# One TensorE queue in source order, reset visit delays, fixed PSUM banks, and both heads of a product in one visit

## The chip, the cores and the metric

One core of one Trainium2 chip runs the whole program. The metric is device time in microseconds (us): the median of several executions. TensorE (PE in the rows) has two records for each product, the weight load (PEld) and the matmul; the other engines are VectorE (DVE), ScalarE (ACT), GpSimd (POOL) and SyncE (SP), which issues most of the DMAs.

## The reference, cut to what matters

One layer of a streaming encoder: two groups of heads on one combined projection, and an output projection.

```python
xn = rms_norm(x, norm_g)
proj = xn @ w_in                       # 2048 x 8320: q, k, v, gates, RWKV rows
q, k = rope(rms_norm(q)), rope(rms_norm(k))
o = softmax(mask(q1 k1)) v - lam * softmax(mask(q2 k2)) v   # two maps a head, 8 heads
for t in tokens:                       # RWKV-7 recurrence, 16 heads of 64
    S = S * w_t + (S a_t) b_t + v_t k_t
    y_t = S r_t
out = concat(att_out, rw_out) @ w_out  # 2048 x 2048
return x + out, k, v, S, last row
```

It is computed for 1024 new frames (64 frames to a chunk) and for 32 frames of a running stream with 256 frames of past.

## The kernel before, in words

The tokens are worked in two halves: A has 544 columns (512 new frames and the 32 of the running stream, projected as 288 + 256 columns), B has 512. For each half there are eight units; unit u is one attention head and one pair of recurrence heads. A unit has eight projections (`proj`, lines 354 to 381): q, k, v, attention gate, three recurrence rows, recurrence gate. Each is 16 blocks of the contraction by three products (`wh xh`, `wh xl`, `wl xh`, which together stand for fp32), so 96 matmuls in A and 48 in B. Ahead of each half stand one norm (`rb_a`, `rb_b`) and one small projection (`lora`). Behind the 16 units come the 16 output projections of A and the 16 of B. All of this is written into the PSUM tag `pj` with three banks.

Everything else runs as *visits* to TensorE between these matmuls. Six streams (lines 167 to 168) are Python generators: `chs` (the recurrence chunk by chunk, `rw_chain`), `dns` (what it needs, `rw_down`), `qks` (norms of q and k, transposes of v), `pos` (`rw_post`), `ats` (`att_task`) and `los` (`rw_decay`). While it writes the program, the planner keeps a clock (`clk`) of the TensorE time it has issued; a stream yields a delay, looked up in the table `LAT` (line 39), and its next visit is written as soon as the clock has passed that delay and one of the stops is reached: `pump()` after every twelve matmuls of a projection in A and six in B, `chs.run()` after every three. `ready` holds a second due time for the shared banks `am` and `Y`. `drain(stream, name)` writes nothing but visits until the named task is through; where none is due it moves its clock on. After the first projection of a unit stands `drain(ats, ("att", u - 1))`: the attention of the unit before must be through. The same is done for the q, k and v tasks one projection after each was added, for `down` and `vread` in the recurrence rows and for the last tasks ahead of the sixteenth output projection.

In the program thus written every engine's order is still open: the Tile scheduler sorts each engine's instructions by the order of the source and by when they are ready in its own timing, TensorE's among them. A delay that is too short in the source therefore costs little: other matmuls are put in front. Each visit allocates its PSUM tile anew from the tags `am`, `Y`, `sc` and `ch`.

The places that the steps below touch: the product BK*AR (lines 753 to 768), for each chunk and head a fp32 matmul of 64 rows by 128 columns of weights and 128 columns of data, two passes each; four chunks of one head make a visit into the bank `Y`. The chunk step (lines 886 to 908): visit c1 `ch<-Sw,AR`, then `RS` (ACT) and `xs` (DVE) from its bank, visit c2 `ch<-xs,TT`, then two copies to `UV`, visit c3 `ch<-UV,MM`, then the new state. Attention in A (`att_task`, `att_finish`): for each of four blocks of queries scores, transposes (`sc<-cst,E`), the product with v (`am<-Vt,E`), and the closing transpose (`am<-cst,os`); then for the running stream `smp0` (`am<-E,qb`), `smp1` (`am<-cmb,E`), `smp2` (`am<-E`) and a last closing transpose.

Of the kernel before, what the change touches and what calls it, by code (L numbers as in the profile page):

```python
# [12 lines left out]
F32R = mybir.dt.float32r  # L13
# [24 lines left out]

LAT = dict(qkA=6246, qkB=2980, vA=9930, vB=9930, finA=1949, finB=3111, sc1A=1400, sc1B=1260, scAA=3566, scAB=3056, sc2A=3181, sc2B=3736, aTA=640, aTB=873, smp0A=2190, smp0B=3000, smp1A=4433, smp1B=7243, smp2A=1452, smp2B=1100, decA=3192, decB=6684, rnA=2646, rnB=1890, msA=8290, msB=8364, ms2A=2463, ms2B=1016, bk0A=1758, bk0B=1724, att0A=4044, att0B=1900, am2A=304, am2B=265, Y2A=1822, Y2B=1994, boA=1350, boB=3075, bktA=2250, bktB=2000, ttA=13941, ttB=14740, t10A=2258, t10B=1343, c0A=1052, c0B=2447, c1A=2162, c1B=1936, c2A=1122, c2B=978, c3A=1014, c3B=1276, postA=6000, postB=4636, dmA=5550, dmB=4110, solveA=31509, solveB=33325, am=900, Y=2208, scA=5863, sc1=2240, sc2=2872)
P3B = 3  # L40
# [6 lines left out]
def build(tc, I, O):  # L47
# [16 lines left out]
    clk = [0.0]  # L64
    ready = {"am": 0.0, "Y": 0.0}

    def am():
        ready["am"] = None
        return PT("am", 1)

    def ym():
        ready["Y"] = None
        return PT("Y", 1)

# [7 lines left out]

    def mm(out, lhsT, rhs, start=True, stop=True):
        n, m = 1, 1
        for d in rhs.shape[1:]:
            n *= d
        for d in lhsT.shape[1:]:
            m *= d
        shaped(lhsT.shape[0], m)
        load = 0.83 * m + 5.0  # L90
        clk[0] += max(0.4375 * n + 6.0, load) if rhs.dtype == F32R else 2 * max(0.84 * n, load)
        PE.matmul(out, lhsT, rhs, start=start, stop=stop)  # L92
# [11 lines left out]
    class Stream:  # L104
# [11 lines left out]
        def due(self):  # L116
            if self.cur is None and not self.q or self.cond is not None and not self.cond():
                return None
            return max(self.at, ready[self.am]) if self.am else self.at

# [5 lines left out]
        def step(self):  # L126
            if self.cur is None:
                if not self.q:
                    return False
                self.cur = self.q.pop(0)  # L130
            if self.cond is not None and not self.cond():
                return False
            if self.due() > clk[0]:
                return False
            self.cond, self.am = None, None
            try:
                y = next(self.cur[1])
            except StopIteration:
                self.done.add(self.cur[0])
                self.cur = None  # L140
                y = 0
            for r in ready:
                if ready[r] is None:
                    ready[r] = clk[0] + LAT[r]
            if callable(y):
                self.cond = y
            elif isinstance(y, tuple):
                self.at, self.am = clk[0] + y[0], y[1]
            else:
                self.at = clk[0] + y  # L150
            return True
# [256 lines left out]
    def lat(key, half):  # L408
        return LAT[key + "AB"[half]]
# [107 lines left out]
    def att_task(half, h, st):  # L517
# [9 lines left out]
        for j in range(4):  # L527
# [10 lines left out]
            if half == 0:  # L538
                sc = PT("sc", 1, (128, 2, 512))
                for c in range(2):  # L540
# [8 lines left out]
            else:  # L549
                for c in range(2):  # L550
                    if c:
                        yield lat("sc1", half) + 2 * nk
                    sc = PT("sc", 1, (128, 2, 512)).rearrange("p a b -> p (a b)")
                    scores(sc, c, qc, segs)
                    V.memset(sc[0:64, nk - 64:nk], NEG)
                    V.tensor_reduce(mx[:, c:c + 1], sc[:, :nk], AX.X, ALU.max)
                    V.tensor_scalar(mx[:, c:c + 1], mx[:, c:c + 1], -SCALE, None, ALU.mult)
                    S.activation(E[c][:, :nk], sc[:, :nk], AF.Exp, bias=mx[:, c:c + 1],
                                 scale=SCALE, accum_out=l[:, c:c + 1])
# [7 lines left out]
            aT = T([128, 8, 128], "E1")  # L567
            pt = PT("sc", 1, (128, 8, 128))
            for kb in range(nb):
# [148 lines left out]
    def rw_down(half, i, sub, st):  # L718
# [35 lines left out]
        for c0 in range(0, cn, 4):  # L754
            m = min(4, cn - c0)
            for h in range(2):
                yield lat(key, half), "Y"
                key = "ms2"
                hr = (low, high)[h]
                p = ym()  # L760
                for j in range(m):
                    mm(p[:, 128 * j:128 * j + 128],
                       BK[hr, c0 + j].rearrange("p a t -> p (a t)"),
                       AR[hr, c0 + j].rearrange("p a t -> p (a t)"))
                V.tensor_tensor(MM[:, c0:c0 + m, h, :].rearrange("p c (x t) -> p c x t", t=64)[:, :, 0:3:2, :],  # L765
                                p[:, :128 * m].rearrange("p (a x t) -> p a x t", x=2, t=64),
                                mask.rearrange("p (x t) -> p x t", x=2).unsqueeze(1).to_broadcast([128, m, 2, 64]),
                                op=ALU.mult)
# [24 lines left out]
        for c0 in range(0, cn, 4):  # L793
            m = min(4, cn - c0)
            yield lat("ms2", half), "Y"
            p = ym()
            for j in range(m):
                tr(p[:, 128 * j:128 * j + 128], BK[:, c0 + j].rearrange("p a t -> p (a t)"), ident)
            for h in range(2):
                S.copy(MM[:, c0:c0 + m, h, 64:128],  # L800
                       p[:, :128 * m].rearrange("p (a b) -> p a b", b=128)[:, :, 64 * h:64 * h + 64])
# [11 lines left out]
    def rw_chain(half, i, sub, st):  # L813
# [8 lines left out]
        yield lat("bk0", half)  # L822
        p = PT("ch", 1)
        for j in range(2):
# [22 lines left out]
        yield max(1500, t_m + lat("tt", half) - clk[0])  # L847
        p = PT("ch", 1)
        for g in range(ng):
            mm(p[32:64, 32 * g:32 * g + 32], MMg[0:32, g, 32:64], u0[:, g, :])  # L850
        S.copy(wt, p[32:64, :32 * ng].rearrange("p (a b) -> p a b", b=32))
        yield lat("t10", half)
        p = PT("ch", 1)
        for g in range(ng):
            mm(p[0:32, 32 * g:32 * g + 32], wt[:, g, :], t01[32:64, g, :])
        pg = p[0:32, :32 * ng].rearrange("p (c h b) -> p c h b", h=2, b=32)
        for h in range(2):
            S.copy(TT[64 * h:64 * h + 32, :, 64 * h + 32:64 * h + 64], pg[:, :, h, :])
        yield lat("t10", half)
        p = PT("ch", 1)  # L860
        for c in range(cn):
# [16 lines left out]
        for c in order:  # L878
# [10 lines left out]
            key = "c1"  # L889
            ch = PT("ch", 1)  # L890
            mm(ch[:, 0:128], AR[:, c].rearrange("p a t -> p (a t)"), Sf)
            RS = T([128, 128], "RS")
            S.copy(RS[high], ch[high, 0:128])  # L893
            xs = T([128, 64], "xs")
            for h in range(2):
                V.tensor_tensor(xs[64 * h:64 * h + 64], ch[low, 64 * h:64 * h + 64], MM[low, c, h, 0:64], op=ALU.add)  # L896
            SP = T([64, 2, 64], "SP")
            for h, hr in enumerate((low, high)):
# [261 lines left out]
```

## Time and profile before

| | us |
|---|---|
| median of 3 runs | 2612.56 (2609.12 to 2618.03) |
| profiled execution | 2613.46 |
| span of its profile | 2611.7 |
| PE busy in it | 2549.7 |
| DVE busy | 1892.0 |
| ACT busy | 1349.6 |

The page gives busy time by engine; a record of a matmul reaches about 0.2 us past the point where the next one begins, so that the distance of two starts is what a matmul costs in a stream. "Idle before" counts only what lies between the end of one record and the start of the next, so a delay shorter than that overhang doesn't show.

### The profile page before, as it was taken

The numbers are of one execution on the slowest core, as the hardware profiler recorded it, in microseconds if no ns is written. First come the engines' busy times: TensorE is split into PE (matmuls) and PEld (weight loads), VectorE is DVE, ScalarE is ACT, GpSimd is POOL, SyncE is SP. The second block draws the span as 40 slices with busy tenths as digits, with TensorE's granted clock in tenths as the row PEclk, the third lists the DMA queues.
The fourth block names the chain that finished last, engine by engine and source line by source line (L and its number), as shares of the span: only waits on it lengthen the run. The fifth ranks groups of instructions, "written<-read, shape, count | busy, mean of one in ns | idle before, by whom it ended". The sixth has DMA issues, their size and how long they took to land. (4 is left out here: it accounts for less than half of the span.)

```text
span 2611.7 us, 49090 instructions
## 1 busy us (share of the span) xinstructions
PE 2549.7 (98%) x17128; PEld 2220.1 (85%) x17128; DVE 1892.0 (72%) x5768; ACT 1349.6 (52%) x3138; POOL 415.1 (16%) x949
## 2 busy tenths in 40 slices
PE   7999999999999999999999999999999999999999
PEld 7999999999898999877777777777777778999887
DVE  7576877777777787788787887788878888753432
ACT  6455555555555655565555555555555556332321
POOL 3211111111111111111111111111111111111000
PEclk9999999999999999999999999999999999999999
DMA  4433332324242524353332323232324244544443
GB/s 156 119 102 94 93 103 84 110 82 115 75 122 80 170 72 122 98 153 100 98 98 87 103 83 106 85 111 81 114 81 115 77 132 118 176 148 140 137 142 108
DMA packets 198665, 286.74 MB, mean 110 GB/s; under 512 B 102097, under 2 KB 115921, under 8 KB 198417
## 3 DMA queue, kind: packets, MB, share of 16 engines
q0 software_dynamic: 51088, 169.12, 21.8%
q1 hardware_dynamic: 147328, 114.47, 15.5%
q8 instruction: 136, 2.23, 0.4%
q14 instruction: 113, 0.92, 0.1%
HBM read 228.11 MB, written 37.51 MB: 102 GB/s over the span
## 5 line engine op out<-in xcount | busy, mean ns | idle before, releaser
L92 PE MATMUL pj<-xh,wh 128*128 128x256 f32 (+2 forms) x3888 | 1294.2, 333 | 7.7 <-ACT xh L248 6.7
L92 PE MATMUL pj<-xl,wh 128*128 128x256 f32 (+2 forms) x3888 | 1274.7, 328 | 5.0 <-DVE xl L249 5.0
L92 PE MATMUL pj<-xh,wl 128*128 128x256 f32 (+2 forms) x3888 | 1272.5, 327 | 1.1 <-DVE wl L225 1.1
L92 PEld LDWEIGHTS pj<-xh,wh 128*128 128x128 f32 x3888 | 735.7, 189 | 61.2 <-ACT xh L248 7.0
L92 PEld LDWEIGHTS pj<-xl,wh 128*128 128x128 f32 x3888 | 736.2, 189 | 52.5 <-DVE xl L249 8.8
L92 PEld LDWEIGHTS pj<-xh,wl 128*128 128x128 f32 x3888 | 735.4, 189 | 52.4 <-DVE wl L225 2.1
L224 ACT CAST wh<-wr 128x512 fp32r<-128x512 f32 x584 | 360.6, 618 | 471.8 <-PE pj L92 420.1
L225 DVE TENSOR_TENSOR wl<-wr,wh 128x512 fp32r<-128x512 f32 x584 | 401.2, 688 | 193.5 <-ACT wh L224 162.9
L231 POOL DMA_DIRECT2D wr<-w_in x517 | 278.3, 538 | 1639.8 <-DVE wl L225 492.2
L786 DVE TENSOR_TENSOR ts<-tm,ts 64x54 f32<-64x54 f32 (+35 forms) x992 | 198.2, 200 | 15.1
L784 DVE TENSOR_TENSOR tm<-ts,ms 64x54 f32<-64x54 f32 (+35 forms) x992 | 197.7, 199 | 14.5 <-DMA ts<-tinit 0.2
L92 PEld LDWEIGHTS ch<-UV,MM 64*64 64x64 f32 (+2 forms) x1632 | 111.5, 145 | 38.1 <-DVE UV L903 9.2
L92 PE MATMUL ch<-UV,MM 64*64 64x64 f32 (+2 forms) x1632 | 128.9, 231 | 8.0 <-DVE UV L846 5.1
L899 ACT ACTIVATE SP<-Sw,PL 64x64 f32<-64x64 f32 x256 | 88.3, 345 | 91.2 <-DVE Sw L908 78.1
L225 DVE TENSOR_TENSOR wl<-MM,wh 128x512 fp32r<-128x512 f32 x64 | 44.0, 689 | 89.1 <-ACT wh L224 89.1
L224 ACT CAST wh<-MM 128x512 fp32r<-128x512 f32 x64 | 39.6, 620 | 128.9 <-PE pj L92 123.3
L896 DVE TENSOR_TENSOR xs<-ch,MM 64x64 f32<-64x64 f32 x272 | 58.6, 216 | 50.2 <-ACT RS L893 45.7
L908 DVE SCALAR_TENSOR_TENSOR Sw<-ch,PL,SP 64x64 f32<-64x64 f32 x256 | 70.7, 276 | 23.2 <-PE ch L92 16.7
L92 PE MATMUL am<-Vt,E 128*128 128x128 f32 (+1 forms) x592 | 84.7, 280 | 1.8 <-ACT wh L224 1.1
L92 PE MATMUL Y<-AR,BK 64*128 64x128 f32 x544 | 84.8, 290 | 0.7 <-DVE MM L765 0.6
L92 PEld LDWEIGHTS Y<-AR,BK 64*128 64x128 f32 x544 | 67.5, 188 | 19.8 <-issue 9.1
L92 PEld LDWEIGHTS am<-Vt,E 128*128 128x128 f32 (+1 forms) x592 | 73.5, 189 | 8.7 <-issue 2.6
(303 smaller groups left out, 3127.9 us busy)
## 6 DMA issues: line engine op xcount, KB each, us to landing
wr<-w_in POOLq DMA_DIRECT2D x517, 256.0 KB, 3.2
wr<-w_out POOLq DMA_DIRECT2D x64, 256.0 KB, 3.6
MM<-w_out POOLq DMA_DIRECT2D x32, 512.0 KB, 4.0
t<-xB SPq DMA_DIRECT2D x32, 256.0 KB
ms<-dm SPq DMA_DIRECT2D x96, 64.0 KB
t<-t SPq DMA_DIRECT2D x64, 68.0 KB
t<-mixd SPq DMA_DIRECT2D x16, 272.0 KB
t<-xA SPq DMA_DIRECT2D x16, 272.0 KB
```

The lines of the kernel that those rows point to most:

```text
L92: PE.matmul(out, lhsT, rhs, start=start, stop=stop)
L224: S.copy(wh, raw)
L225: V.tensor_tensor(wl, raw, wh.bitcast(F32), op=ALU.subtract)
L231: q.dma_start(raw, wsrc[:, g * 512:(g + 1) * 512].rearrange("p (k f) -> p k f", k=4))
L784: V.tensor_tensor(tm, ts_[:, 0:qn, s:s + 1].to_broadcast([R * nb, qn, m]), ms[:, s:s + 1, s + 1:32].to_broadcast([R * nb, qn, m]), op=ALU. ...
L786: V.tensor_tensor(ts_[:, 0:qn, s + 1:32], tm, ts_[:, 0:qn, s + 1:32], op=ALU.add)
L896: V.tensor_tensor(xs[64 * h:64 * h + 64], ch[low, 64 * h:64 * h + 64], MM[low, c, h, 0:64], op=ALU.add)
L899: S.activation(SP[:, h, :], S_[hr, h, :], AF.Copy, scale=PL[hr, 0, gc:gc + 1])
L908: V.scalar_tensor_tensor(S_[hr, h, :], ch[low, 192 + 64 * h:256 + 64 * h], PL[low, h, gc:gc + 1], SP[:, h, :], ALU.mult, ALU.add)
```

## The change

TensorE gets its instructions in the order of the source (`tc.manual_schedule` for PE alone); the other engines are sorted as before. The table of delays is reset: most grow, a few shrink, and there are new entries for two steps that had shared one. The banks `am`, `Y`, `sc` and `ch` are allocated once and kept. BK*AR takes both heads in one visit: the matmuls alternate between rows 0 to 63 and rows 64 to 127, head 0 into `Y` and head 1 into `am`; the planner counts them at half the time. In the chunk step `xs` is now written ahead of `RS`.

```diff
-LAT = dict(qkA=6246, qkB=2980, vA=9930, vB=9930, finA=1949, finB=3111, sc1A=1400, sc1B=1260, scAA=3566, scAB=3056, sc2A=3181, sc2B=3736, aTA=640, aTB=873, smp0A=2190, smp0B=3000, smp1A=4433, smp1B=7243, smp2A=1452, smp2B=1100, decA=3192, decB=6684, rnA=2646, rnB=1890, msA=8290, msB=8364, ms2A=2463, ms2B=1016, bk0A=1758, bk0B=1724, att0A=4044, att0B=1900, am2A=304, am2B=265, Y2A=1822, Y2B=1994, boA=1350, boB=3075, bktA=2250, bktB=2000, ttA=13941, ttB=14740, t10A=2258, t10B=1343, c0A=1052, c0B=2447, c1A=2162, c1B=1936, c2A=1122, c2B=978, c3A=1014, c3B=1276, postA=6000, postB=4636, dmA=5550, dmB=4110, solveA=31509, solveB=33325, am=900, Y=2208, scA=5863, sc1=2240, sc2=2872)
+LAT = dict(qkA=6246, qkB=2980, vA=9930, vB=9930, finA=3400, finB=3400, sc1A=1400, sc1B=2600, scAA=6400, scAB=3056, sc2A=3181, sc2B=4100, aTA=1200, aTB=2000, smp0A=3600, smp0B=3000, smp1A=9000, smp1B=7243, smp2A=1452, smp2B=1100, decA=3192, decB=6684, rnA=2646, rnB=6200, msA=8290, msB=8364, ms2A=2600, ms2B=3000, bk0A=7300, bk0B=6000, att0A=4044, att0B=1900, am2A=2100, am2B=265, Y2A=1950, Y2B=1950, boA=1350, boB=3075, ttA=27000, ttB=25500, t10A=1000, t10B=1000, c0A=1300, c0B=1700, c1A=2500, c1B=2300, c2A=2500, c2B=2500, c3A=1700, c3B=1800, postA=6000, postB=4636, dmA=5550, dmB=4110, solveA=31509, solveB=33325, am=1500, Y=2208, scA=5863, sc1=2240, sc2=2872, x0A=1000, x0B=1000, bkA=2600, bkB=3000)
...
+    held = {}
+
+    def bank(tag, shape=(128, 512)):
+        if tag not in held:
+            held[tag] = PT(tag, 1, shape)
+        return held[tag]
+
     def am():
         ready["am"] = None
-        return PT("am", 1)
+        return bank("am")
...
-        clk[0] += max(0.4375 * n + 6.0, load) if rhs.dtype == F32R else 2 * max(0.84 * n, load)
+        clk[0] += (max(0.4375 * n + 6.0, load) if rhs.dtype == F32R else 2 * max(0.84 * n, load)) / ways
...
         for c0 in range(0, cn, 4):
             m = min(4, cn - c0)
+            yield lat(key, half), "Y", "am"
+            key = "ms2"
+            ps2 = (ym(), am())
+            for j in range(m):
+                for h, hr in enumerate((low, high)):
+                    mm(ps2[h][:, 128 * j:128 * j + 128],
+                       BK[hr, c0 + j].rearrange("p a t -> p (a t)"),
+                       AR[hr, c0 + j].rearrange("p a t -> p (a t)"), ways=2)
             for h in range(2):
-                yield lat(key, half), "Y"
-                key = "ms2"
-                hr = (low, high)[h]
-                p = ym()
-                for j in range(m):
-                    mm(p[:, 128 * j:128 * j + 128],
-                       BK[hr, c0 + j].rearrange("p a t -> p (a t)"),
-                       AR[hr, c0 + j].rearrange("p a t -> p (a t)"))
                 V.tensor_tensor(MM[:, c0:c0 + m, h, :].rearrange("p c (x t) -> p c x t", t=64)[:, :, 0:3:2, :],
...
-            ch = PT("ch", 1)
+            ch = bank("ch")
             mm(ch[:, 0:128], AR[:, c].rearrange("p a t -> p (a t)"), Sf)
-            RS = T([128, 128], "RS")
-            S.copy(RS[high], ch[high, 0:128])
             xs = T([128, 64], "xs")
             for h in range(2):
                 V.tensor_tensor(xs[64 * h:64 * h + 64], ch[low, 64 * h:64 * h + 64], MM[low, c, h, 0:64], op=ALU.add)
+            RS = T([128, 128], "RS")
+            S.copy(RS[high], ch[high, 0:128])
...
     with tile.TileContext(nc) as tc:
-        build(tc, I, O)
+        with tc.manual_schedule(engines={mybir.EngineType.PE}):
+            build(tc, I, O)
```

## Rows read from the trace of the kernel before

**Rows 1.** The page: the span, and busy time by engine.
```profile
span 2611.7 us, 49090 instructions
PE 2549.7 (98%) x17128; PEld 2220.1 (85%) x17128; DVE 1892.0 (72%) x5768; ACT 1349.6 (52%) x3138; POOL 415.1 (16%) x949
```
**Rows 2.** Busy time by stretch: length, PE, PEld, DVE, ACT, POOL, granted clock, DMA share, GB/s.
```profile
0.00:37.20 37.20, 24.54 (x121) 21.30 (x122) 29.95 (x47) 22.84 (x37) 16.66 (x27) 0.86 0.61 205
22.00:31.00 9.00, 7.90 (x32) 7.24 (x32) 8.68 (x9) 2.61 (x5) 4.55 (x4) 0.50 0.16 50
40.00:60.00 20.00, 18.92 (x143) 17.81 (x141) 10.39 (x19) 14.85 (x23) 3.60 (x9) 1.00 0.37 107
```
**Rows 3.** Timeline of PE around one visit: start us, length us.
```profile
2236.06 0.29 PE L92 MATMUL pj<-xh,wl 128*128 128x288 f32 x1
2236.28 1.16 PE L92 MATMUL Y<-AR,BK 64*128 64x128 f32 x8
...
2237.61 0.30 PE L92 MATMUL pj<-xl,wh 128*128 128x288 f32 x1
2237.75 0.29 PE L92 MATMUL pj<-xh,wl 128*128 128x288 f32 x1
```
**Rows 4.** Groups by line and form: busy us, mean ns | idle before, by releaser.
```profile
L92 PE MATMUL Y<-AR,BK 64*128 64x128 f32 x544 | 84.8, 290 | 0.7 <-DVE MM L765 0.6
L92 PE MATMUL ch<-xs,TT 128*128 128x64 f32 x272 | 54.3, 281 | 12.2 <-DVE xs L896 7.0 <-issue 2.1 <-ACT E L571 1.1
```
**Rows 5.** Timeline of PE, a visit whose products use two column halves.
```profile
631.00 0.68 PE L92 MATMUL ch<-UV,MM 64*64 64x64 f32 x16
```
**Rows 6.** Timeline of PE around a chunk visit that waits.
```profile
700.27 0.28 PE L92 MATMUL pj<-xh,wl 128*128 128x256 f32 x1
700.62 0.46 PE L92 MATMUL ch<-Sw,AR 128*128 128x128 f32 x2
```
**Rows 7.** What VectorE waited for ahead of `xs`: us, times.
```profile
  ACT RS L893: 47.8, 42
```
**Rows 8.** Timeline of PE at the start.
```profile
21.66 0.61 PE L92 MATMUL pj<-xl,wh 128*128 128x288 f32 x1 [2.29 <-DVE xl L249]
...
37.23 0.62 PE L92 MATMUL am<-asg,p 128*128 128x272 f32 x2
```
**Rows 9.** Timeline of DVE at the start.
```profile
32.17 0.69 DVE L225 TENSOR_TENSOR wl<-wr,wh 128x512 fp32r<-128x512 f32 x1 [1.49 <-ACT wh L224]
35.51 0.72 DVE L273 TENSOR_TENSOR asg<-asg,p 128x544 f32<-128x544 f32 x1
```
**Rows 10.** Timeline of PE, end of attention in a unit of A, and the projection behind.
```profile
563.81 0.25 PE L92 MATMUL am<-kb,qb 128*64 128x32 f32 x2
573.12 0.81 PE L92 MATMUL am<-cmb,E 64*128 64x32 f32 x6
581.90 0.24 PE L97 MATMUL am<-cst,os 32*128 32x32 f32 x1
583.59 0.29 PE L92 MATMUL pj<-xh,wh 128*128 128x288 f32 x1
```
**Rows 11.** Timeline of DVE, what `smp1` there needs.
```profile
565.63 0.45 DVE L595 TENSOR_REDUCE sx<-am 64x1 f32<-64x288 f32 x1
568.24 0.29 DVE L602 TENSOR_SCALAR cmb<-cst,sx,cvec 64x32 f32<-64x32 f32 x1
```
**Rows 12.** Timeline of ACT, what the last closing transpose there needs.
```profile
576.70 0.27 ACT L504 ACTIVATE os<-am 32x128 f32<-32x128 f32 x1 [0.62 <-PE am L92]
577.65 0.36 ACT L509 ACTIVATE os<-am,sm 32x128 f32<-32x128 f32 x1
```
**Rows 13.** Timeline of PE, end of attention in a unit of B.
```profile
1558.48 1.95 PE L92 MATMUL am<-Vt,E 128*128 128x128 f32 x16
1563.26 0.27 PE L97 MATMUL am<-cst,os 128*128 128x128 f32 x1
```
**Rows 14.** Instructions of the norm ahead of half B: ns min/median/max, first and last start.
```profile
L92 PE MATMUL am<-p,p x8: 270/274/377, 1144.3 to 1147.6; 128*128 128x128 f32 x8
```

More of the change, by code (lines that the diff above doesn't have):

```diff
@@ L65, in build, with scores2 @@
     ready = {"am": 0.0, "Y": 0.0}
+    held = {}
[3 more added lines that the diff above has]
+        return held[tag]
     def am():
         ready["am"] = None
-        return PT("am", 1)
+        return bank("am")
     def ym():
         ready["Y"] = None
-        return PT("Y", 1)
+        return bank("Y")
+    def scores2():
+        return bank("sc", (128, 2, 512))
     mode = [(128, 128)]
@@ L81, in shaped, with mm @@
             mode[0] = now
-    def mm(out, lhsT, rhs, start=True, stop=True):
+    def mm(out, lhsT, rhs, start=True, stop=True, ways=1):
         n, m = 1, 1
@@ L118, in due @@
                 return None
-            return max(self.at, ready[self.am]) if self.am else self.at
+            return max(self.at, *(ready[a] for a in self.am)) if self.am else self.at
         def run(self):
@@ L147, in step @@
             elif isinstance(y, tuple):
-                self.at, self.am = clk[0] + y[0], y[1]
+                self.at, self.am = clk[0] + y[0], y[1:]
             else:
@@ L538, in att_task @@
             if half == 0:
-                sc = PT("sc", 1, (128, 2, 512))
+                sc = scores2()
                 for c in range(2):
@@ L552, in att_task @@
                         yield lat("sc1", half) + 2 * nk
-                    sc = PT("sc", 1, (128, 2, 512)).rearrange("p a b -> p (a b)")
+                    sc = scores2().rearrange("p a b -> p (a b)")
                     scores(sc, c, qc, segs)
@@ L567, in att_task @@
             aT = T([128, 8, 128], "E1")
-            pt = PT("sc", 1, (128, 8, 128))
+            pt = scores2().rearrange("p a (b t) -> p (a b) t", t=128)
             for kb in range(nb):
@@ L755, in rw_down @@
             m = min(4, cn - c0)
-            for h in range(2):
-                yield lat(key, half), "Y"
-                key = "ms2"
-                hr = (low, high)[h]
-                p = ym()
-                for j in range(m):
-                    mm(p[:, 128 * j:128 * j + 128],
-                       BK[hr, c0 + j].rearrange("p a t -> p (a t)"),
-                       AR[hr, c0 + j].rearrange("p a t -> p (a t)"))
+            yield lat(key, half), "Y", "am"
[6 more added lines that the diff above has]
+                       AR[hr, c0 + j].rearrange("p a t -> p (a t)"), ways=2)
+            for h in range(2):
                 V.tensor_tensor(MM[:, c0:c0 + m, h, :].rearrange("p c (x t) -> p c x t", t=64)[:, :, 0:3:2, :],
-                                p[:, :128 * m].rearrange("p (a x t) -> p a x t", x=2, t=64),
+                                ps2[h][:, :128 * m].rearrange("p (a x t) -> p a x t", x=2, t=64),
                                 mask.rearrange("p (x t) -> p x t", x=2).unsqueeze(1).to_broadcast([128, m, 2, 64]),
@@ L794, in rw_down @@
             m = min(4, cn - c0)
-            yield lat("ms2", half), "Y"
+            yield lat("bk", half), "Y"
             p = ym()
@@ L822, in rw_chain @@
         yield lat("bk0", half)
-        p = PT("ch", 1)
+        p = bank("ch")
         for j in range(2):
@@ L847, in rw_chain @@
         yield max(1500, t_m + lat("tt", half) - clk[0])
-        p = PT("ch", 1)
+        p = bank("ch")
         for g in range(ng):
@@ L852, in rw_chain @@
         yield lat("t10", half)
-        p = PT("ch", 1)
+        p = bank("ch")
         for g in range(ng):
@@ L858, in rw_chain @@
             S.copy(TT[64 * h:64 * h + 32, :, 64 * h + 32:64 * h + 64], pg[:, :, h, :])
-        yield lat("t10", half)
-        p = PT("ch", 1)
+        yield lat("x0", half)
+        p = bank("ch")
         for c in range(cn):
```

## The prediction

> **What bounds the kernel now.** I read the page first, then busy time by stretch, then TensorE's groups by form, then the timeline around single visits. The page says that TensorE is busy for 2549.7 of 2611.7 us [rows 1], so the end of the kernel is TensorE's own queue: every matmul taken out of it and every wait in it counts in full, and every wait put into it as well. The other engines (DVE 72%) matter by when they release a visit. TensorE is idle for 62.0 us in all [rows 1]; the first 37.2 us hold 12.7 of that, since it is busy for 24.54 there [rows 2]. The other 49.3 us lie in short waits at visits. That is less than what they cost: at 700.27 a projection matmul starts, the visit behind it at 700.62 [rows 6], where the mean distance in a dense stretch is 18.92 / 143 = 0.132 us [rows 2]; of the 0.22 us lost, the record of the matmul (0.28 us long) leaves only 0.07 visible as idle. So visits come a little too early as a rule, and the sorted queue hides the rest by putting projection matmuls in front.
>
> **BK*AR, both heads in one visit.** From the last projection matmul before a visit to the second behind it, 2236.06 to 2237.61, are 1.55 us; two of these matmuls cost 2 x 0.14, so the visit costs 1.27 us [rows 3]. With eight passes at some 0.115 us (first to last start is 1.16 less a record's 0.29, seven gaps of 0.12 [rows 3, 4]) that leaves 0.35 us for going in and out. The 544 passes [rows 4] are 64 visits of eight and 16 of two (subs of 4 and 5 chunks in A, 4 and 4 in B). After: 32 of sixteen and 8 of four. Whether row halves run side by side no row of before shows, as each visit used one half. The nearest row is a visit that uses two column halves: 16 passes in 0.68 us, less a record's overhang of some 0.2, are 0.03 us each [rows 5], where 64 columns alone would cost half of 0.115, 0.058; there two passes do run at once. I take that for row halves too: a double visit then costs what a single one does and some 0.1 more, so 32 x 1.17 + 8 x 0.5 = **-42 us**. If they don't, only the entries are saved: 40 x 0.35 = -14. The Trainium skill, TensorEngine Tiling (Array Packing), section PSUM Pressure, says that different row tiles must not write one PSUM bank at the same time; the change uses two banks, as that asks. No run here shows that rule, and the sum doesn't use it.
>
> **Source order and later visits.** With TensorE in source order the planner's delays decide. The new ones for the chunk steps (c1 2.5, c2 2.5, c3 1.7 in A) are longer by 0.3 to 1.4 us, and `xs` no longer stands behind `RS`, for which VectorE waited 47.8 us in 42 cases [rows 7]. The recurrence has room for that: it isn't what the projections wait for, as the wait on `xs` in front of TensorE is 12.2 us in 272 passes [rows 4]. So most of the 49.3 us of idle time behind the start goes, and the hidden part (0.15 us in perhaps 170 of the 408 chunk visits, 25 us) pays for the visits that are still late, which now hold the whole queue. I take **-50 us**; bounds -25 (half stays) and -75 (both go). The banks that are kept cost nothing: the same readers must be through before the next write; that holds unless the kept tile brings a second semaphore wait, which is inside these bounds.
>
> **The start.** `rb_a` stands ahead of all projections in the source. In the trace its first matmul runs at 37.23 [rows 8], behind 121 projection matmuls that the sorter put in front [rows 2]. In source order TensorE waits for the last sum of squares, 35.51 + 0.72 = 36.23 [rows 9], and then has those 121 to do: 121 x 0.132 = 16.0 us. It can start 0.8 us earlier than 37.23, or 4.7 if the weight casts, one of which ran ahead of the last sums after a wait of 1.49 us [rows 9], are held back by full buffers. So +11 to +15, and up to 4.5 more (half of the 9.00 us at clock 0.50 [rows 2]) if it starts at the lower of its two levels, 1.2 GHz. I take **+14**. `rb_b` has four rounds of matmul, copy, same bank, spread over 1144.3 to 1147.6 [rows 14] among other matmuls; alone in the queue they cost 3.3 less 8 x 0.11 = **+2.5** (0 to 3).
>
> **The drain of attention.** This is the price of the change. In a unit of A the last closing transpose is at 581.90 and the next projection begins at 583.59 [rows 10]: attention ends 1.7 us ahead of the drain point as it is. The new table adds 4 x 2.83 (scA) + 5 x 1.45 (fin) + 1.41 + 4.57 (smp0, smp1) + 4 x 0.56 (aT) = 26.8 us to its delays. Some 25 us of planned delays then fall behind the drain point, so `smp0`, `smp1`, `smp2` and the last closing transpose stand in the queue with no projection between. TensorE doesn't wait for the planned time there but for the data. For `smp1` that took from 564.06 to 568.53 = 4.5 us with a loaded VectorE [rows 10, 11] (its visit came at 573.12, 9.1 us later, for want of the bank), and for a closing transpose from 576.70 to 578.01 = 1.3 us [rows 12]; `smp0` has its data already; `smp2`, two small copies, I estimate at 0.5. That is 6.3 us; chunk visits that the drain lets through fill some of it. I take 4.5 us of idle time a unit, bounds 2 and 12 (9.1 and a loaded 2.8). Eight units: **+36** (16 to 96). In B the closing transpose is at 1563.26 [rows 13], at the drain point, and the table adds 4 x (1.34 + 0.36 + 1.13 + 0.29) = 12.5 us: the last product and closing transpose fall behind it. Between these lay 1563.26 - 1560.43 = 2.8 us [rows 13], at best 1.3 [rows 12]; with part of the wait ahead of the product I take 2.5 a unit (1.3 to 5), seven units, **+17.5** (9 to 35). What is queued behind is the q evacuation and all projections; no other engine has work that needs TensorE meanwhile.
>
> **The sum**, against the profiled execution's 2613.46 us (0.9 above the median): -42 - 50 + 14 + 2.5 + 36 + 17.5 = -22, so 2591.5; I say **2591**.
>
> **The rivals.**
> The drains cost more, and the kernel is slower: with 12 us a unit in A and 4 in B they take 96 + 28 = 124 in place of 53.5, and the time is 2661. It decides at the point where the drains eat the gain, 92 - 16.5 = 75.5 us over 15 drains, 5.0 us each. For it: closing transposes and `smp1` waited that long in this trace, and chunk visits in between have waits of their own. Against it: the long ones were queues on VectorE and ACT that a standing TensorE doesn't feed. Clock: after an idle 2.29 us at 21.66 [rows 8] the granted clock was 0.50 from 22 to 31 us [rows 2]; a fall like that in each drain of A would add 8 x 4.5 = 36, so 2697. The Trainium skill, TensorE: Matmul & The Clock Gate, section HAM oscillation, warns of just this, of idle time between bursts that throttles the clock again and again; the stretch from 22 to 31 us agrees.
> Row halves don't overlap: -14 in place of -42, 2619.
> The waits all go and the drains are nearly free, because attention, no longer queued behind early work, comes in time: -42 - 75 + 14 + 16 + 9 = -78, 2535.
> The sorted order was near the source's anyway, so that the order itself changes nothing: then only the merged visits count, 2571; it is part of the forecast's range.
>
> **How the numbers follow.** Forecast (2555 to 2604): 0.40. Nearly free drains (below 2555): 0.13. No overlap (near 2619): 0.13. Costly drains (above): 0.34. About 0.3%, 8 us, is what a measurement of this kernel can tell from no change: faster 0.40 + 0.13 = 0.53, same 0.13, slower 0.34. Cases of both signs hold the chance, so the range takes in both: 2530 (all waits gone, drains at their lower bound) to 2685 (costly drains, some lower clock); the forecast's own range is 2555 to 2604.
>
> **What would show it.** BK*AR: visits of sixteen passes, some 1.4 us from first start to the next projection, not 2.1. Source order: idle ahead of `ch` visits down from what it is, `rb_a` as TensorE's first matmuls, at 32 to 37 us. Drains: in each unit a stretch of some 10 us after the first projection in which TensorE runs only visits, with `am<-cmb,E`, `am<-E` and `am<-cst,os` the ones that wait, 4 to 6 us idle in A and 2 to 3 in B; and the granted clock there. Wrong would be: attention through ahead of the drain point; idle time in a drain above 5 us; passes of the two halves starting 0.11 us apart.

## The result, and the profile after

The changed kernel takes 2826.07 us (median of 4 runs, 2821.76 to 2828.24) where the kernel before takes 2612.64 beside it (2609.12 to 2618.03): a ratio of 1.081, interval 1.079 to 1.084. It is slower by 213 us. The forecast was 2591 and the range ended at 2685, so size and sign were both wrong.

The page of the changed kernel: span, busy time by engine, then TensorE's busy share and its granted clock in 40 equal slices, in tenths.

```profile
span 2822.7 us, 48865 instructions
PE 2544.6 (90%) x17128; PEld 2262.1 (80%) x17128; DVE 1915.7 (68%) x5768; ACT 1349.0 (48%) x3138; POOL 422.6 (15%) x949
PE   4989898998989798988989898989898989899999
PEclk9989899998989898989999999999899999999999
```

TensorE does the same 17128 matmuls and is busy as long as before, 2544.6 against 2549.7 us [rows 1]. Its idle time went from 62.0 to 2822.7 - 2544.6 = 278.1 us, which is more than the whole difference. In the busy time two things nearly cancel: the merged visits take time out, and the granted clock, 0.943 on the mean where it was 0.995, puts time in. The same matmuls with the same merged visits are busy for 2519.5 us at clock 0.988 in the run `merged_sorted` below, so some 25 us here may be the clock's (an estimate from these two runs). The dips in the first row come once a unit. One of them, in the busy time by stretch (length, PE, PEld, DVE, ACT, POOL, granted clock, DMA share, GB/s): the start, the 16 us ahead of the second projection of unit 4, that place itself, the 14 us behind it, and the same place in a unit of B.

```profile
0.00:37.20 37.20, 3.52 (x9) 2.70 (x9) 28.48 (x46) 21.81 (x35) 14.53 (x24) 1.00 0.54 184
615.00:631.00 16.00, 15.38 (x126) 15.17 (x126) 12.43 (x40) 9.11 (x23) 1.66 (x4) 1.00 0.35 90
631.00:651.00 20.00, 10.26 (x50) 6.88 (x49) 18.31 (x72) 8.80 (x26) 1.50 (x5) 0.64 0.18 55
651.00:665.00 14.00, 14.00 (x103) 14.00 (x103) 5.10 (x19) 4.04 (x11) 1.08 (x2) 0.91 0.42 108
1999.00:2020.00 21.00, 9.95 (x44) 8.23 (x43) 17.22 (x66) 9.30 (x25) 0.74 (x2) 0.65 0.30 91
```

For 20 us TensorE runs 50 matmuls and is busy half the time, while VectorE is busy 18.31 us. The granted clock is 0.64 there, a mixture of its two levels, 1.2 and 2.4 GHz. The timeline of TensorE in that drain (start, length, and in brackets the idle time ahead and what ended it):

```profile
631.14 0.28 PE L102 MATMUL pj<-xh,wl 128*128 128x256 f32 x1
632.75 0.33 PE L107 MATMUL am<-cst,os 128*128 128x128 f32 x1 [1.33 <-ACT os L519]
634.35 0.64 PE L107 MATMUL am<-cst,Yt 128*128 128x128 f32 x3 [1.27 <-DVE asg L524]
...
636.10 0.25 PE L102 MATMUL am<-kb,qb 128*64 128x32 f32 x2
...
639.05 1.27 PE L102 MATMUL am<-cmb,E 64*128 64x32 f32 x6 [2.06 <-DVE tm L794]
642.72 0.55 PE L102 MATMUL Y<-AR,BK 64*128 64x128 f32 x1 [2.40 <-DVE ts L796]
...
646.28 1.06 PE L102 MATMUL am<-E 128*32 128x128 f32 x4 [1.34 <-DVE MM L775]
...
650.47 0.31 PE L107 MATMUL am<-cst,os 32*128 32x32 f32 x1 [0.38 <-DVE MM L775]
650.71 0.61 PE L102 MATMUL pj<-xh,wh 128*128 128x288 f32 x1
```

From the last matmul of the first projection to the first of the second are 19.6 us. Adding up the idle time between these two matmuls gives 4.7 to 12.0 us in each of the 15 drains, 139 in all, and 7.5 more behind the last projection of A, around the norm `rb_b`; in the kernel before no idle time shows at these places. The start has 33.7. The remaining 98 us lie ahead of visits inside the units. TensorE's waits by releaser (us in total, times, longest), the largest first:

```profile
PE am L107 <- DVE Yt L947: 35.3, 18, 3.9
PE am L102 <- DVE p L317: 33.7, 1, 33.7
PE ch L102 <- ACT RS L906: 30.7, 20, 4.7
PE am L107 <- ACT os L519: 22.3, 15, 3.6
PE ch L102 <- DVE UV L913: 21.4, 11, 3.7
PE sc L107 <- DVE tm L794: 20.0, 6, 3.6
PE Y L102 <- DVE ts L796: 17.0, 6, 3.2
```

And two of TensorE's groups, which answer to [rows 4] (busy, mean ns, idle before by releaser):

```profile
L102 PE MATMUL Y<-AR,BK 64*128 64x128 f32 x272 | 52.9, 340 | 20.5 <-DVE ts L796 17.0 <-DVE MM L775 1.9 <-DVE BK L760 1.5
L102 PE MATMUL ch<-xs,TT 128*128 128x64 f32 x272 | 48.9, 262 | 30.8 <-ACT RS L906 30.7
```

The waits are spread over recurrence, attention and what precedes it, with no single line to blame. Where `xs` waited behind `RS` on VectorE before, it now waits for TensorE (35.3 us in 32 cases), and the product behind it waits for `RS`: 30.8 us of idle time where it was 12.2. (Of the 47.8 us in [rows 7] 45.7 were VectorE's, in 40 cases; the other 2.1 lay ahead of TensorE's weight load.)

### The profile page after: what moved, and what is told of

It reads as the page before. It is cut to its first block, busy times and chain, and to the rows that moved or that the text cites. A ratio compares the mean times of both kernels' runs of the same rounds, so it can differ in the third digit from the quotient of the medians.

```text
span 2822.7 us, 48865 instructions
## 1 busy us (share of the span) xinstructions
PE 2544.6 (90%) x17128; PEld 2262.1 (80%) x17128; DVE 1915.7 (68%) x5768; ACT 1349.0 (48%) x3138; POOL 422.6 (15%) x949
## 4 chain that ended last, share of the span: by engine, by line
PE 69%; DVE 18%; ACT 6%; issue 4%; DMA 2%; POOL 0%; SPq 0%; DVEq 0%; ACTq 0%; POOLq 0%
PE pj L102 54%; PE ch L102 5%; PE am L102 4%; DVE wl L235 3%; DVE ts L796 2%; DVE tm L794 2%; PE Y L102 2%; PE sc L102 1%; PE sc L107 1%; PE am L107 1%; ACT wh L234 1%; DVE E L573 1%; DVE t L472 1%; DVE Sw L918 1%; PE Y L107 1%
## 5 line engine op out<-in xcount | busy, mean ns | idle before, releaser
L102 PE MATMUL pj<-xh,wh 128*128 128x256 f32 (+2 forms) x3888 | 1332.1, 343 | 3.4 <-DVE t L361 3.4
L102 PEld LDWEIGHTS pj<-xh,wl 128*128 128x128 f32 x3888 | 744.4, 191 | 58.0 <-DVE wl L235 0.4
L102 PEld LDWEIGHTS pj<-xh,wh 128*128 128x128 f32 x3888 | 746.1, 192 | 51.9 <-DVE t L361 4.3
L102 PEld LDWEIGHTS pj<-xl,wh 128*128 128x128 f32 x3888 | 746.7, 192 | 40.7
L794 DVE TENSOR_TENSOR tm<-ts,ms 64x54 f32<-64x54 f32 (+35 forms) x992 | 198.5, 200 | 18.6 <-DMA Qd<-Qd 1.0
L796 DVE TENSOR_TENSOR ts<-tm,ts 64x54 f32<-64x54 f32 (+35 forms) x992 | 198.5, 200 | 18.1
L102 PE MATMUL am<-Vt,E 128*128 128x128 f32 (+1 forms) x592 | 94.0, 311 | 5.5 <-DVE ts L796 3.1
L102 PEld LDWEIGHTS am<-Vt,E 128*128 128x128 f32 (+1 forms) x592 | 85.2, 220 | 13.7 <-issue 9.5
L904 DVE TENSOR_TENSOR xs<-ch,MM 64x64 f32<-64x64 f32 x272 | 58.6, 215 | 39.9 <-PE ch L102 35.3
L102 PEld LDWEIGHTS ch<-xs,TT 128*128 128x128 f32 x272 | 46.3, 192 | 42.9 <-ACT RS L906 38.4
L568 ACT ACTIVATE E<-sc,sm 128x640 f32<-128x640 f32 (+3 forms) x64 | 61.1, 954 | 37.9 <-DVE sm L567 37.3
```

The costliest lines, as they stand in the source:

```text
L794: V.tensor_tensor(tm, ts_[:, 0:qn, s:s + 1].to_broadcast([R * nb, qn, m]), ms[:, s:s + 1, s + 1:32].to_broadcast([R * nb, qn, m]), op=ALU. ...
L796: V.tensor_tensor(ts_[:, 0:qn, s + 1:32], tm, ts_[:, 0:qn, s + 1:32], op=ALU.add)
```

## The experiments

Three theories stood against each other. **O**: the fixed order itself costs the time; whatever a visit waits for, TensorE now waits too. **P**: the new, longer delays cost it, by pushing attention past the drain point. **Q**: in the drains TensorE stands behind VectorE's queue, above all the 62 operations of each triangular solve. Times without an interval are those of one execution; the kernel before had 2609.6 to 2619.0 us beside them.

**Order and delays apart.** Four kernels: only the order held; the whole change with the old delays; the whole change with the order left to the scheduler; and the last with the old delays as well.

```diff
     with tile.TileContext(nc) as tc:          # order_alone: this edit in the kernel before
-        build(tc, I, O)
+        with tc.manual_schedule(engines={mybir.EngineType.PE}):
+            build(tc, I, O)
-LAT = dict(... c1A=2500 ...)                  # old_delays: this edit in the changed kernel
+LAT = dict(... c1A=2162 ...)                  # all old values; x0 as t10, bk as ms2
```

> The kernel before with TensorE in source order and nothing else. Theory P: the plan of before has next to no empty time, so 2640 to 2720 us: the start costs 15, early visits cost the rest. Rival O: 2800 or more. Against the run with old delays it shows what kept banks and merged visits give in source order: 30 to 45 us by the prediction's term.

> The whole change but for the table: source order on TensorE, kept banks, both heads in one visit, and the delays of before (the two new entries at the values they shared). Theory P (the lengthened delays plan empty time into the drains, and source order makes TensorE stand there): the fifteen stretches of some 20 us behind each first projection shrink to a few us and most of the loss goes, 2600 to 2690 us, while visits that now come too early wait. Rival O (source order itself costs, whatever the delays, since no other matmul can be put in front of a wait): the time stays near 2800.

> The whole change with the new delays, but TensorE sorted by the scheduler as before. Theory P: the sorter puts projection matmuls into the drains, so the time is near or below before, 2570 to 2630 us. If the long delays cost by themselves (attention late whoever orders it), 2700 or more.

> Kept banks, both heads of BK*AR in one visit and xs ahead of RS, with the sorted order and the delays of before. The prediction's term for the merged visits is -42 us if the row halves overlap and -14 if not: 2570 or 2599 us.

Measured: order alone 2870.9; whole change with old delays 2828.4; whole change without the order 2654.4; that with old delays 2604.8 (median of 10 executions, ratio 0.9975, interval 0.9962 to 0.9988). The order costs 2870.9 - 2612.6 = 258 us on the kernel before, 2828.4 - 2604.8 = 224 on the changed one with old delays and 2826.1 - 2654.4 = 172 with the new ones. The new delays cost 2654.4 - 2604.8 = 50 us where the order is sorted and nothing (-2) where it is held. So O holds and P doesn't. The 50 us of the new delays in sorted order were not followed up. The page of the whole change without the order:

```profile
span 2652.6 us, 48829 instructions
PE 2527.5 (95%) x17128; PEld 2220.1 (84%) x17128; DVE 1894.3 (71%) x5768; ACT 1344.8 (51%) x3138; POOL 419.6 (16%) x949
```

Its idle time is 125.1 us where the changed kernel has 278.1. So of the 170 us between the two spans 153 are idle time and 17 are busy time, at a mean clock of 0.943 in place of 0.974. Where the waits are does depend on the table. With the old delays the drains, the one behind the last projection of A included, hold 19 us of idle time, not 147, and the largest releaser of TensorE's waits in that kernel is

```profile
PE ch L102 <- ACT RS L906: 81.0, 76, 3.1
```

More of the waits sit ahead of the chunk visits there (121.7 us of idle time ahead of `ch`, with the new table 79.5), and the total is much the same: 286 us, with the new table 278.

**Between the tables.**

```diff
-LAT = dict(... finA=3400, scAA=6400, smp1A=9000, c1A=2500 ...)
+LAT = dict(... finA=2674, scAA=4983, smp1A=6716, c1A=2331 ...)   # halfway: means; att_old: attention's old
```

> The changed kernel with each delay at the mean of the old and the new value; the order of TensorE's work stays the source's. The new delays give 2826 us and the old ones gave 2828 us. Theory P (the two tables err on two sides: the old ones are too short and leave waits in the visits, the new ones too long and leave drains; what lies between is clearly better): 2700 to 2770 us. Theory O (what the fixed order costs is the visits' own waiting, which a delay only moves from the visits to the end of attention): 2790 to 2840 us.

> The changed kernel with the old delays for attention's visits and the new ones for everything else. Theory P (attention's longer delays push its end past the unit's last projection, and that alone makes the drains; the recurrence has room for its own longer delays): the drains behind the first projection go, of which TensorE stood some 150 us idle, and the time is 2650 to 2720 us. Theory O (what the fixed order costs is waiting that a delay moves from one place to another): 2790 to 2850 us, with the idle time in attention's own visits and in the recurrence.

Measured: 2846.4 and 2851.1 us. Both are above either table. The idle time in the drains falls from 147 to 82 us halfway, but the total rises to 2844.6 - 2545.3 = 299. Old attention delays with new ones for everything else are the slowest of the four tables, though the 5 us to halfway are no more than single executions can differ by. P falls a second time, and so does my sentence that the recurrence has room: the longer delays outside attention cost 2851.1 - 2828.4 = 23 us against the old table.

**VectorE's solves.** The first of 31 steps is kept, so the solves are left incomplete.

```diff
-        for s in range(31):
+        for s in range(1):
```

> The changed kernel, but each triangular solve does only the first of its 31 steps on VectorE (62 operations of some 0.2 us become 2, in each of 32 solves; about 385 us of VectorE's work is left out, and the output is not the reference's). All matmuls, transfers, delays and the order of TensorE's work stay. The changed kernel's own time is 2826 us. Theory Q (in the long drains TensorE stands behind VectorE's queue, where the solve steps lie ahead of what the drained visits need; VectorE was busy 18.3 us of the 20 us of one drain): the drains shorten from about 20 us towards TensorE's own 10 us in them, 15 x 5 to 10 us, and the time falls by 75 to 150 us, to 2675 to 2750 us. Theory O (with its order fixed TensorE waits out each visit's own chain of operations, whoever else is busy): VectorE's other work is of no account, the time falls by less than 40 us, to 2785 to 2826 us.

> The kernel before with the same work left out of the solves (the first of 31 steps is kept). Its time is 2610 us. Theory Q and theory O alike: where other matmuls can go in front of a wait, VectorE's queue costs little, so the time falls by 0 to 20 us, to 2590 to 2610 us. If it falls as far as the changed kernel does with the same edit, the solve steps cost both alike and say nothing on the change.

Measured: 2760.6 for the changed kernel, 65 us less, and 2545.6 for the kernel before, 67 us less than 2612.6 (73 less than the run beside it). For the changed kernel neither bracket was hit, Q's 75 to 150 or O's under 40. For the kernel before the forecast of at most 20 failed, and its other branch came true: both kernels lose alike, so the solve steps say nothing on the change. The difference of the two kernels, 2760.6 - 2545.6 = 215 us, is what it was with whole solves, 213. In the changed kernel the drains still hold 126 us of idle time. So Q does not explain the change. What it found in the kernel before is told at the end.

**The start.**

```diff
-    rb_a()
-    ready["am"] = clk[0]
     load_rope(0)
     Lt = lora(0, wpre)       # and rb_a() behind the projection inside lora
```

> The changed kernel with the rowblock of the first half put back behind the first adapters' projection, where the kernel before issues it in effect; all else stays. In the changed kernel TensorE ran this rowblock at 33.7 us of the span and the first unit began at 50.3 us, 17 us later than in the kernel before. If the start's term is right and stands by itself: 17 us less, 2805 to 2815 us. If the later start is taken up by waits that would come anyway: 2820 to 2830 us.

Measured: 2812.5 us, 13.6 less, inside the first bracket. The start's term stands by itself.

**The merged visit and the fixed banks, each alone.** `single_head` puts the visit by head back into the changed kernel; the other two put one part into the kernel before.

```diff
-            yield lat(key, half), "Y", "am"       # single_head (reversed in pair_sorted)
-            ps2 = (ym(), am())
...
+            for h in range(2):
+                yield lat(key, half), "Y"
...
+                p = ym()
...
-        return PT("am", 1)                        # banks_sorted: also Y, sc, ch, and xs ahead of RS
+        return bank("am")
```

> The changed kernel with BK*AR done again head by head, in two visits of bank Y each, all else as changed (source order, new delays, fixed banks). The changed kernel's time is 2826 us. If the merged visit is worth what its term says even in the changed kernel (42 us: half the occupancy of 544 matmuls of 64 rows): 2860 to 2875 us. If it saves TensorE's time but TensorE then waits as much longer, because the chain through VectorE and ScalarE stays: 2815 to 2840 us. If needing bank am as well, which attention uses, costs more than it saves: below 2815 us.

> The kernel before with the merged BK*AR visit alone (both heads, rows in alternating halves, into banks Y and am); old delays, the planner's order sorted as before, banks allocated per visit. The kernel before takes 2612.6 us; with fixed banks and the exchanged copy as well it took 2604.8 us. By the term of the prediction: 42 us less, 2570 us, or 14 us less, 2599 us, if the two row halves do not overlap. If the occupancy falls but the time is set by what the visits wait for: 2598 to 2612 us. If the merge gave more than the 8 us and the fixed banks took some back: 2585 to 2598 us.

> The kernel before with the fixed banks and the exchanged copy of the recurrence alone; BK*AR head by head, old delays, sorted order. The prediction set these parts at nothing: 2606 to 2619 us. If allocating a bank once takes freedom from the sorted order: 2620 us and above. If the 8 us of the version with all three came from here: 2600 to 2606 us.

Measured: 2840.2 without the merged visit in the changed kernel, so the merge is worth 14 us there, although the drains of units 9 to 15 hold only 4.8 to 6.0 us of idle time each without it, where the changed kernel has 9.2 to 12.0. Alone in the kernel before it gives 2600.2 us, ratio 0.9948 (0.9925 to 0.997), which is 13.6 us less. Fixed banks and the exchanged copy alone give 2620.3, ratio 1.0036 (1.0018 to 1.0053): by the ratio they cost 9 us where I had nothing. TensorE's groups of the merged visit in `pair_sorted` (busy, mean ns, idle before):

```profile
L92 PE MATMUL Y<-AR,BK 64*128 64x128 f32 x272 | 41.6, 288 | 0.0
L92 PE MATMUL am<-AR,BK 64*128 64x128 f32 x272 | 41.4, 288 | 0.5 <-DVE asg L514 0.5
```

A record's length hides the overlap; the distance of the starts shows it. Summed over all passes, it falls from 544 x 147 ns = 79.9 us to 272 x 133 + 272 x 35 = 45.8. That is 34 us less of TensorE's time, near the term of 42. But in this kernel the span fell by 9.3 us only (2602.4), as the idle time rose from 62.0 to 86.2.

**Which instructions stand behind which.** The changed kernel again, with the source's order held for all of TensorE's instructions except one kind, by a token that keeps those that carry it in order.

```diff
+    def held_order(x):
+        if not (inside[0] == 'chain'):   # att_free: 'att'; proj_free: is None (not in a visit)
+            tc.stamp_issue_order_token(x.ins, "PE")
...
-        PE.matmul(out, lhsT, rhs, start=start, stop=stop)
+        held_order(PE.matmul(out, lhsT, rhs, start=start, stop=stop))
...
-        with tc.manual_schedule(engines={mybir.EngineType.PE}):
-            build(tc, I, O)
+        build(tc, I, O)
```

> The changed kernel with the source's order held for all of TensorE's instructions except those of the recurrence's chain (one visit per chunk), which the planner may place later, as the kernel before lets it for all. The same source takes 2826 us with everything held and 2654 us with nothing held. Counting the projection matmuls ahead of each visit, the chain's visits are those that the sorted order moves back the most (27 to 31 projection matmuls in the middle; attention's 0 to 5). Theory O1 (what TensorE stands behind is mostly the recurrence's chain, held in the source's place): 2655 to 2720 us. Theory O2 (attention's visits, which end late and are drained behind the first projection, cost as much by themselves): 2740 to 2826 us.

> The same with attention's visits free to be placed later and everything else, the recurrence's chain too, in the source's order. Theory O1: the chain still holds TensorE up, 2780 to 2826 us. Theory O2 (the drains of attention's visits behind the first projection are the loss: 15 of about 20 us, with 147 us of idle TensorE): 2660 to 2740 us.

> The same with the order held among all visits (attention, recurrence, adapters) but the projections' matmuls free to go in front of them. If what the fixed order lacks is projection matmuls to put in front of a waiting visit, this gets most of the 172 us back: 2654 to 2700 us. If it is visits of one task that have to pass those of another: 2740 to 2826 us.

> The whole change with the old delays, the source's order held for all but the recurrence's chain. The same source takes 2828 us with everything held and 2605 us with nothing held. Theory O1: 2605 to 2680 us. Theory O2: 2740 to 2828 us.

Measured: with the recurrence's chain free 2794.4 us, 32 less; with attention free 2830.7, nothing; with the projections free 2646.1, 180 less, which is all that the order costs with these delays (172). With old delays a free chain gives 2724.7, 104 of 224. `proj_free` frees all that stands outside the visits, the norms ahead of the halves too, so the start's term is among its 180 us: its first matmul runs at 6.79 us, the changed kernel's at 33.68. Between O1 and O2 the runs don't decide: the free chain falls into O2's bracket, free attention just above O1's, the free chain with old delays between the two. They say little on whose visits cost the time, because a freed kind hardly moved. Counting the projection matmuls ahead of each visit matmul, a free chain puts `ch<-UV,MM` 0.6 later than the changed kernel on the mean, where the sorted order with the same delays puts it 14.6 later; free attention puts `am<-E` 0.8 later, the sorted order 66.9. With the projections free the mean over all visits is 21.6. So the visits may keep their order among themselves; what was lost are projection matmuls put in front of a visit that waits. The end of attention of the same unit, from its last full closing transpose to the last one of all, in the kernel with free projections (`proj_free`), by stretch:

```profile
597.40:617.80 20.40, 20.33 (x147) 17.65 (x148) 18.40 (x66) 9.16 (x21) 2.96 (x7) 1.00 0.33 96
```

And on TensorE's timeline there, with the projection matmuls left out but for one:

```profile
597.41 0.33 PE L112 MATMUL am<-cst,os 128*128 128x128 f32 x1
...
603.72 0.80 PE L107 MATMUL am<-cmb,E 64*128 64x32 f32 x6
604.45 0.38 PE L107 MATMUL pj<-xl,wh 128*128 128x256 f32 x1
...
613.03 0.62 PE L107 MATMUL am<-E 128*32 128x128 f32 x4
...
617.50 0.25 PE L112 MATMUL am<-cst,os 32*128 32x32 f32 x1
```

This is the reading on which the explanation rests. The chain takes 20.1 us here, and 17.7 in the drain of the changed kernel (632.75 to 650.47). VectorE is busy 18.40 us here and 18.31 there. The visits are no faster and VectorE no freer, but TensorE runs 147 matmuls in place of 50, at clock 1.00 in place of 0.64.

One more kernel, the kernel before with the merged visit alone and the order held among visits:

> The kernel before with the merged BK*AR visit alone, old delays and banks per visit, and the source's order held among all visits, with the projections' matmuls free to go in front of them. With nothing held the same source gave a ratio of 0.9948 to the kernel before (2600 us). If visits need not pass each other: 2595 to 2606 us, a ratio of 0.993 to 0.998. If with the old, shorter delays a visit that is held behind another's wait costs more than with the new ones: 2610 to 2680 us.

Measured: 2611.2 us, ratio 0.9995 (0.998 to 1.001), where the same without held visits gave 0.9948. So with the old, shorter delays the order among the visits is worth some 12 us, small beside 258. The fastest complete version is the kernel before with the merged visit alone, 2600 us.

## Why the prediction was wrong

**Source order** (-50 predicted) is the step that failed. I counted the waits that longer delays would remove and took the waits that the order lays bare for about 25 us. It cost 172 us with the new delays, and that includes the start and the drains. The idle time behind the start, of which most was to go, rose from 49.3 us to 278.1 - 33.7 = 244.4. The step said that the sorted queue hides the rest of the waits by putting projection matmuls in front, and then priced only the part still visible. How much it hides can be counted: for each visit matmul I took how many projection matmuls run ahead of it in `order_alone`, and how many in the kernel before, whose source is the same. 3426 of 5464 have more ahead in the sorted order, 6 have fewer; the mean is 17, for the chunks' `ch<-UV,MM` 31. At 0.132 us a matmul [rows 2] these 31 are 4 us. The rival that the sorted order is near the source's falls with this count. The count shows that waits are hidden and at which visits; it doesn't give their price, which only the runs with the order held told.

**The drains** (+36 and +17.5 predicted): place and cause were right, the size was not: 139 us of idle time in place of 53.5. What the drains cost by themselves stays open, since the old table leaves 19 us of idle time there and the kernel is as slow. Units 1 to 7 have 7.7 to 9.7 us of idle time each, not 4.5, and units 9 to 15 have 9.2 to 12.0, not 2.5; all are above the 5.0 that I had named as the turning point. The term that was mis-sized is the chain: I added data times of single steps to 6.3 us where 17.7 pass. Of these steps `smp1` took less than I had (2.7 us from the end of `am<-kb,qb` to `am<-cmb,E`, in place of 4.5), but from the end of `am<-cmb,E` to `am<-E` (`smp2`, which I estimated at 0.5) 6.0 us passed in the drain shown above. VectorE in that gap:

```profile
642.64 0.17 DVE L620 COPY E<-am 32x32 f32<-32x32 f32 x1
644.80 0.69 DVE L775 TENSOR_TENSOR MM<-Y,cst 128x512 f32<-128x512 f32 x1
645.55 0.68 DVE L775 TENSOR_TENSOR MM<-am,cst 128x512 f32<-128x512 f32 x1
```

The second of the two copies ended at 642.81, so the data was there. But ahead of `am<-E` stood the merged visit of BK*AR, begun at 642.72, half of it in the bank `am`; VectorE had read that bank at 646.23, and `am<-E` ran at 646.28. The change itself had put that visit into attention's bank. I argued that a standing TensorE doesn't feed the queue on VectorE. But VectorE was busy 18.31 of 20 us there, and 18.40 in the same place without a drain; 37 of its 72 operations in the drain are steps of a solve (L794, L796). The lower clock, which I had put beside the rival of costly drains, came: 0.64 in the drain, 0.91 in the 14 us behind it, 0.943 over the span where it was 0.995. The Trainium skill, TensorE: Matmul & The Clock Gate, section HAM oscillation, warns of idle time between bursts of matmuls that throttles the clock again and again, there for waits on DMA; the trace agrees, with waits on VectorE and ScalarE. The rival of costly drains named a part of the mechanism, but even with the clock it ended at 2697: it still booked the waits inside the units as a gain, where 98 us of idle time stand after the change.

**The recurrence has room** was wrong: new delays with attention's old ones gave 2851, all old ones 2828. I had read room from the 12.2 us of idle time that show, but ahead of `ch<-xs,TT` the sorted order had put 21 more projection matmuls than the source, on the mean.

**BK*AR** (-42 predicted): the halves do run at once, two passes start together every 0.11 us at full clock, and the occupancy fell by 34 us. (The term's own sum, 32 x 1.17 + 8 x 0.5, is 41.4.) What failed is the step before the sum, that every matmul taken out counts in full. It counted by 13.6.

**The fixed banks** (nothing predicted) cost 9 us in sorted order, together with the exchanged copy; which of the two it is was not tried.

**The start** (+14): 13.6 measured. The first matmul came at 33.68, within the 32 to 37 named. **rb_b** (+2.5): the waits between its four rounds add up to 2.3 us, with 4.4 ahead of the first.

The way from before to after, by the measured steps: 2612.6, merged visit with banks and copy -8, new delays +50, order with start and drains +172, which gives 2826. Taken the other way round, the order costs 224 and the delays nothing.

## What to carry to other kernels

A queue that is 98% busy because a scheduler fills its waits says nothing of how long these waits are; before fixing its order, count how far the scheduler moves instructions from the source's place. A large count (here 17 matmuls on the mean) says that the idle time left is no bound for what a fixed order costs; the price itself took a run with the order held. If an order is to be fixed, fix it among the dependent visits and leave the independent bulk of the work free to go between them: here that took away all of the 172 us. A table of delays can move waits from the visits to a barrier and back, but four tables came out within 25 us of each other.

## What the runs showed that I had not expected

TensorE's busy time hides waits even where it is 98%. The page of the kernel before with short solves:

```profile
span 2543.8 us, 47049 instructions
PE 2507.8 (99%) x17128; PEld 2213.9 (87%) x17128; DVE 1617.4 (64%) x3848; ACT 1346.9 (53%) x3138; POOL 418.0 (16%) x949
```

No matmul was taken out, and the span fell by 67.9 us: 26 us of idle time and 41.9 us of "busy" time (2549.7 to 2507.8). A record reaches past the start of the next one, so waits shorter than that overhang count as busy. Two other things changed with it and were not separated. The mean granted clock was 0.999 in place of 0.995, which over 2550 us can be worth some 10 of the 42 us (an estimate). And the sorted order differed: 3187 of the 5464 visit matmuls have another number of projection matmuls ahead. The Trainium skill, Perfetto Trace Analysis, says in its opening note that matmul busy time is a bad metric for how close a kernel is to roofline, because matmuls are pipelined; this run agrees that it is a bad measure, as the busy time fell by 42 us with no matmul taken out.

Two products of 64 rows into two banks ran side by side: in the changed kernel a pass started every 0.11 us in each bank, as one alone did before [rows 3, 4]. TensorE's timeline in one merged visit, which takes 1.09 us from its first start to the next projection matmul, where I had named some 1.4:

```profile
1229.31 0.37 PE L102 MATMUL Y<-AR,BK 64*128 64x128 f32 x1
1229.32 0.37 PE L102 MATMUL am<-AR,BK 64*128 64x128 f32 x1
...
1229.97 0.27 PE L102 MATMUL Y<-AR,BK 64*128 64x128 f32 x1
1229.98 0.27 PE L102 MATMUL am<-AR,BK 64*128 64x128 f32 x1
1230.08 0.27 PE L102 MATMUL Y<-AR,BK 64*128 64x128 f32 x1
1230.09 0.27 PE L102 MATMUL am<-AR,BK 64*128 64x128 f32 x1
...
1230.40 0.39 PE L102 MATMUL pj<-xh,wh 128*128 128x256 f32 x1
```
